# A planner that follows which bank is released first, and prices accumulator reads and narrow products

## The chip, the cores and the metric
The kernel runs on one core of one Trainium2 chip. The metric is the device time of one execution in microseconds. The core has five engines with queues of their own: PE (TensorE, with its weight loads shown as PEld), DVE (VectorE), ACT (ScalarE), POOL (GpSimd) and SP (SyncE, which here issues every DMA).

## The reference, cut to what matters
One layer of a hybrid decoder for a prompt of 512 tokens and for 8 decoding sequences of 4 new tokens each, all with D_MODEL 2048 in fp32:

```
z = rms_norm(x, g) @ w_in                      # 2048 -> 6144: q, k, v, g_A, u, g_B
a = dilated_prompt(q, k, v)                    # 16 heads x 64, three (window, dilation) patterns
a = dilated_sample(q, concat(cache_k, k), concat(cache_v, v), buf)   # the decoding rows
p = pool_mix(u)                                # trailing means over 2/4/8/16, 256x256 maps
h = x + concat(a * silu(g_A), p * silu(g_B)) @ w_out
y = rms_norm(h, final_norm_g)
# also returned: keys, values and pool history, among them the updated caches
# (8 x 2048 x 1024, keys and values), which are the old ones moved on by 4 rows
```

## The kernel before, in words
**Two stages.** The first stage multiplies the 544 tokens by w_in: 48 blocks of 128 output channels (`order`: q, k, v, g for eight head pairs, then u and p for the pooling), each the sum of 16 products over d. A product is three times two matmuls of 272 columns, since a weight and an input are each split into a high and a low part (`w_split`, `x_split`, `product`). Attention and pooling run in between. The second stage multiplies by w_out in 512-column blocks with all eight PSUM banks, then normalises and writes y.

**What is woven in.** The four main PSUM banks `mm` belong to the blocks (and to the pooling maps). Two banks, tag `aux`, serve everything else that PE does for the attention: `B`, query rows copied over the partitions for the decoding keys (`query_rows`, names `aux<-qm,oh`; DVE reads it in three multiplications `tmp<-kv,aux`, spread out over time); `S`, prompt scores (`prompt_scores`, `aux<-kHH,qS` and `aux<-kL,qS`; DVE reads it once, in `tensor_tensor_reduce`, which the profile calls CUSTOM_DVE_ANT_0 plus an accumulator read); `T`, transposed probabilities (`prompt_values`, `aux<-cst,P`; ACT copies it to `PT`); and transposes of new rows (`aux<-cst,zr`), of outputs (`aux<-cst,ov`) and of the decoding softmax. Banks `O` and `OS` collect attention outputs. The DMA side streams the caches through a ring `kv` of 7 buffers (plus one, `kvx`).

**What sets the order.** The program's order on each engine is fixed when the kernel is built, by a planner inside it. `Paced` wraps each engine: each call advances a modelled time `t` of that engine by a cost (`_pe_cost`, `_dve_cost`, `_act_cost`), not before its inputs are ready in the model (`Clock.ready`). Tasks are Python generators; `tick`, run after each product (`between`), resumes those whose condition holds at the modelled PE time `pe.t`. So an attention matmul takes its place in PE's in-order stream where the model says that its inputs will be there. `after(engine)` waits until `pe.t` has passed that engine's time plus MARGIN (0.4); `idle(dve)` waits until DVE's modelled backlog is under 0.2.

**Banks.** `bank()` first holds one of the two `aux` places (`hold`, by count), then makes the tile, then `vacant` waits until `pe.t` is past the time at which the model thinks that the tile's place came free, plus BANK (0.15). That time is the `floor` which `Clock.new` notes: the last recorded access of the tile made `bufs` tiles earlier in the same ring.

```
old = self.done[ring[-bufs]] if len(ring) >= bufs else ([], [])
floor = max([e[4] for es in old for e in es], default=0.0)
```

`kv_advance` asks `next_free` the same question of the `kv` ring before it issues a cache load on SP. `BULK_LEAD` paces 224 transfers that copy the caches from HBM to HBM: one is issued after a product while the modelled DMA time lies 2 us behind `pe.t`; those that are left are spread over the second stage.

Of the kernel before, what the change touches and what calls it, by code (L numbers as in the profile page):

```python
# [49 lines left out]
class Clock:  # L50
# [4 lines left out]
           ("POOL", "POOL"): 0.1}  # L55

    def __init__(self):
        self.done, self.rings = {}, {}

    def pool(self, pool, bufs=1):  # L60
        return PacedPool(self, pool, bufs)

    def new(self, t, bufs):
        ring = self.rings.setdefault(t.tensor.tag, [])
        old = self.done[ring[-bufs]] if len(ring) >= bufs else ([], [])
        floor = max([e[4] for es in old for e in es], default=0.0)
        ring.append(t.tensor.name)
        self.done[t.tensor.name] = ([(0, 128, 0, 1 << 30, floor, "")], [])

    def free(self, t):  # L70
        return self.done[t.tensor.name][0][0][4]

    def next_free(self, tag, bufs):

        ring = self.rings.get(tag, [])
        old = self.done[ring[-bufs]] if len(ring) >= bufs else ([], [])
        return max([e[4] for es in old for e in es], default=0.0)

    def box(self, x):
# [105 lines left out]
def _pe_cost(name, args, kw):  # L185
    n = _free(args[0])
    if name == "transpose":
        return 0.11
    if args[1].dtype == F32R:
        return 0.006 + max(n, 256) / 2264  # L190
    t = 4 * max(n, 64) / 2400
    return t / 4 if kw.get("tile_position") is not None else t / (2 if args[1].shape[-1] == 64 else 1)


def _dve_cost(name, args, kw):
    n = _free(args[1] if name == "tensor_reduce" else args[0])
    fast = name in ("tensor_scalar", "tensor_copy") and args[1].space != PSUM
    return 0.07 + n / (1920 if fast else 960) + (0.06 if name == "tensor_scalar" else 0.0)


def _act_cost(name, args, kw):
    t = _free(args[0]) / 1200 + (0.052 if args[1].space == PSUM else 0.094)
    if not isinstance(kw.get("scale", 1.0), float):
        t += 0.094
    return t + (0.094 if "accum_out" in kw else 0.0) + (0.094 if "bias" in kw else 0.0)


def _pool_cost(name, args, kw):
# [4 lines left out]
def kernel(ctx: ExitStack, tc: tile.TileContext, xT, xtok, ck, cv, stT, w_in, w_pool, w_out,  # L213
                           cst, fg, y, kpT, vpT, ppT, ks, vs, psT):
    nc = tc.nc
    clock = Clock()
# [35 lines left out]
    def bank(shape=(128, 512)):  # L252
        yield from hold("aux")
        b = px.tile(list(shape), F32, name="aux", bufs=2)
        yield from vacant(b)
        return b

    def vacant(t):
        free = clock.free(t)
# [109 lines left out]
    xr = {}  # L369
# [12 lines left out]
    def x_split(d):  # L382
        act.activation(xH[d], xr[d], AF.Copy, scale=gcol[:, d:d + 1])
        dve.scalar_tensor_tensor(xL[d], xr[d], gcol[:, d:d + 1], xH[d].bitcast(F32), ALU.mult, ALU.subtract)
        k = d % 2
        sq = sums[k] if d < 2 else per.tile([128, NT], F32, name="sq", tag=f"mixP{2 + d % 6}")
        act.activation(sq, xr[d], AF.Square)
        if d >= 2:
            squares.append((k, sq))

# [18 lines left out]
    def rstd_rows():  # L409
        yield after(dve, pool)  # L410
        b = yield from bank()
        for t in range(5):
            n = 128 if t < 4 else 32
            for k in range(2):
                pe.matmul(b[:n, t:t + 1], sums[k][:, 128 * t:128 * t + n], ones, start=(k == 0), stop=(k == 1))
        r5 = per.tile([128, 5], F32, name="r5")
        dve.memset(r5, 1.0)
        dve.tensor_copy(r5[:, 0:4], b[:, 0:4])
        dve.tensor_copy(r5[:32, 4:5], b[:32, 4:5])
        give("aux")  # L420
        pow_rstd(r5, r5, 128)
        yield after(pool)
        yield 1.5
        b = yield from bank()
        for t in range(4):
            pe.transpose(b[:, 128 * t:128 * t + 128], r5[:, t:t + 1].to_broadcast([128, 128]), ident)
        dve.tensor_copy(rstd[:, 0:512], b)
        give("aux")
        b = yield from bank()
        pe.transpose(b[:, 0:32], r5[:32, 4:5].to_broadcast([32, 128]), ident[:32, :32])  # L430
        dve.tensor_copy(rstd[:, 512:544], b[:, 0:32])
        give("aux")
        normed.append(1)

    normed = []
# [54 lines left out]
    def ev_q(p, ps):  # L490
        pr[p] = {"P": {}}
        z = yield from scaled(ps, -0.125)
        yield after(dve)
        Q, a = divmod(p, 2)
        b = yield from sample_rows(z)
        yield after(pe)
        if Q > 1 and Q - 2 not in softened:
            yield lambda: Q - 2 in softened
        qm = quad(Q)["q"]
        cols = slice(128 * a, 128 * a + 128)  # L500
        act.activation(qm[0:32, cols], b, AF.Copy)
        yield after(act)
        dve.tensor_tensor(qm[32:64, cols], b, qm[0:32, cols].bitcast(F32), ALU.subtract)
        give("aux")
        if a == 1:
            quad(Q)["ready"].add("q")
        st = []
        for s in range(2):
            o, n = 64 * s, 64 - 64 * s
            t = yield from slot("qS", F32R)  # L510
            act.activation(t[o:o + 64, :NP], z[o:o + 64, :NP], AF.Copy)
            st.append(t)
        yield after(act)
        for s in range(2):
            o, n = 64 * s, 64 - 64 * s
            dve.tensor_tensor(st[s][n:n + 64, :NP], z[o:o + 64, :NP], st[s][o:o + 64, :NP].bitcast(F32),
                              ALU.subtract)
        give("zr")
        pr[p]["qS"] = st

    def ev_k(p, ps):
# [3 lines left out]
        b = yield from sample_rows(z)  # L525
        yield after(pe)
        dve.tensor_copy(quad(Q)["k"][:, 128 * a:128 * a + 128], b)
        give("aux")
        if a == 1:
            yield after(dve)  # L530
            quad(Q)["ready"].add("k")
# [25 lines left out]
    def ev_v(p, ps):  # L557
        z = yield from scaled(ps)
        yield after(dve)
        Q, a = divmod(p, 2)  # L560
        b = yield from sample_rows(z)
        yield after(pe)
        dve.tensor_copy(quad(Q)["v"][:, 128 * a:128 * a + 128], b)
        give("aux")
        vt = yield from slot("vt")
        b = yield from bank()
        for j in range(4):
            pe.transpose(b[:, 128 * j:128 * j + 128], z[:, 128 * j:128 * j + 128], ident)
        yield after(pe)
        act.activation(vt[:, :NP], b, AF.Copy)  # L570
        give("aux")
        dma.start(nc.sync, vpT[128 * p:128 * p + 128, :], z[:, :NP])
        give("zr")
        yield after(act)
        pr[p]["vt"] = vt
        if a == 1:
            quad(Q)["ready"].add("v")
            kv_new()
            dma.start(nc.sync, vs[:, 2044:2048, 256 * Q:256 * Q + 256], quad(Q)["v"])
# [24 lines left out]
    def prompt_scores(p):  # L604
        st = pr[p]
        for i in range(4):
# [3 lines left out]
            for s in range(2):  # L610
# [4 lines left out]
                if i == 3:  # L615
# [5 lines left out]
                n = at.tile([128, 4], F32, name="n", bufs=6)  # L621
                dve.tensor_tensor_reduce(P[:, :nk], S[:, :nk], c[:, C_NBP + NP - nk:C_NBP + NP], 1.0, BIG,
                                         ALU.add, ALU.min, n[:, 0:1])
                give("aux")
                Ps.append(P)
                ns.append(n)
                yield after(dve)
# [9 lines left out]
    def prompt_values(p):  # L637
        st = pr[p]
        for i in range(4):
# [5 lines left out]
            for s in range(2):  # L645
                PT = yield from slot("PT")
                T = yield from bank()
                for j in range(i + 1):
                    pe.transpose(T[:, 128 * j:128 * j + 128], Ps[s][:, 128 * j:128 * j + 128], ident)
                give("P")  # L650
                yield after(pe)
                act.activation(PT[:, :nk], T[:, :nk], AF.Copy)
                give("aux")
                PTs.append(PT)
            yield after(act)
            if "vt" not in st:
# [43 lines left out]

    def kv_done(*ns):
        for n in ns:
            give(kv_tag.pop(n))

    def kv_load(n):
        Q, kv, b, h = parts[n]
# [1 line left out]
        cols = slice(256 * Q, 256 * Q + 256)  # L708
        tag = kv_next()
        taken[tag] += 1  # L710
        kv_tag[n] = tag
        if tag == "kvx":
            t = per.tile([128, NS, 256], F32, name="kvx", tag="mixP01")
        else:
# [4 lines left out]
            src = cache[b, 1536:1920, cols].rearrange("(a r) e -> a r e", r=4)  # L719
        else:  # L720
            src = cache[b:b + 4, 1920:2048, cols].rearrange("b r e -> r b e")
        kv_key[tag] = t.tensor.tag
        kv_time[n] = dma.start(nc.sync, t if h == 2 else t[0:96], src)
        kvt[n] = t
# [40 lines left out]
    def sample_all():  # L765
# [7 lines left out]
        for Q, kv, b in units:  # L773
# [7 lines left out]
            if kv == 0:  # L781
# [6 lines left out]
                for i in (0, 2):  # L788
# [5 lines left out]
                    for seg, nr, t in ((0, 96, tA), (1, 100, tB), (2, 128, tC)):  # L794
# [7 lines left out]
                        dve.tensor_tensor(tmp[:nr], kt, B[:nr], ALU.mult)  # L802
                        lo = 16 * b + 4 * i
                        pieces.append((SCs[Q][:nr, seg, lo:lo + 8], tmp[:nr].rearrange("p i (h d) -> p (i h) d", d=64)))
                    give("aux")
                kv_done(n, n + 1, *([nc4] if last else []))
                if b == NB - 1:
                    while pieces:
# [37 lines left out]
    def sample_softmax(Q):  # L846
# [10 lines left out]
        sb = lent("tmp")[:, :324]  # L857
        n = at.tile([128, 4], F32, name="n", bufs=6)
        dve.tensor_tensor_reduce(sb, T[:, :324], c[:, C_NBS:C_NBS + 324], 1.0, BIG, ALU.add, ALU.min, n[:, 0:1])
        give("aux")  # L860
        yield after(dve)
        act.activation(sb, sb, AF.Exp, bias=n[:, 0:1], scale=-1.0, accum_out=n[:, 1:2])
        yield after(act)
# [10 lines left out]
        act.activation(PA[:96, 0:128], T[:96, 0:128], AF.Copy)  # L874
        act.activation(PA[:100, 128:256], T[:100, 128:256], AF.Copy)
        act.activation(PA[:, 256:384], T[:, 256:384], AF.Copy)
        give("aux")
        yield after(act)
        sampled.add(Q)

# [2 lines left out]
    def sample_near(Q, b4, C):  # L883
# [1 line left out]
        yield after(pe)  # L885
        ov = sa.tile([128, 256], F32, name="ov", bufs=1)
        act.activation(ov, C, AF.Copy)
        give("aux")
        yield after(act)
        T = yield from bank()  # L890
        for k in range(2):
# [3 lines left out]
        for s in range(2):  # L895
# [1 line left out]
            Tb = T[lo:lo + 64, s:s + 255]  # L897
            dve.tensor_copy(mixS[lo:lo + 64, 2 * Q:2 * Q + 2, 4 * b4:4 * b4 + 16].rearrange("p k (j i) -> p k j i", i=NS),
                            bass.AP(tensor=Tb.tensor, offset=Tb.offset, ap=[Tb.ap[0], [130, 2], [32, 4], [4, 4]]))
        give("aux")  # L900
        near.add((Q, b4))

    def sample_out(Q, b2, O):
# [14 lines left out]
        for s in range(2):  # L918
# [3 lines left out]
            Tb = T[lo:lo + 64, s:s + 511]  # L922
            dve.tensor_tensor(o, bass.AP(tensor=Tb.tensor, offset=Tb.offset,
                                         ap=[Tb.ap[0], [130, 2], [256, 2], [32, 4]]), o, ALU.add)
        give("aux")
        for s in range(2):
            lo = 64 * s
            o = mixS[lo:lo + 64, 2 * Q:2 * Q + 2, at8]
# [463 lines left out]
```

## Time and profile before

| | us |
|---|---|
| median of 3 runs | 983.32 (982.81 to 984.39) |
| the profiled execution | 982.86 |
| its span, first to last instruction | 981.1 |
| PE busy in the span | 943.6 (96%) |
| DVE busy | 679.5 (69%) |
| ACT busy | 317.0 (32%) |

The span leaves out some 1.8 us at the ends of the execution. PE's busy time counts matmuls with modelled, overlapping ends, so a start-to-start distance says more of its rate than a duration does. All calls through the planner's wrapper carry line L149, all DMAs L174: the groups are told apart by the names of the tiles, as out<-in. A wait is put down to the instruction that ended it.

### The profile page before, as it was taken

The numbers are of one execution on the slowest core, as the hardware profiler recorded it, in microseconds if no ns is written. First come the engines' busy times: TensorE is split into PE (matmuls) and PEld (weight loads), VectorE is DVE, ScalarE is ACT, GpSimd is POOL, SyncE is SP. The second block draws the span as 40 slices with busy tenths as digits, with TensorE's granted clock in tenths as the row PEclk, the third lists the DMA queues.
The fourth block names the chain that finished last, engine by engine and source line by source line (L and its number), as shares of the span: only waits on it lengthen the run. The fifth ranks groups of instructions, "written<-read, shape, count | busy, mean of one in ns | idle before, by whom it ended". The sixth has DMA issues, their size and how long they took to land.

```text
span 981.1 us, 17768 instructions
## 1 busy us (share of the span) xinstructions
PE 943.6 (96%) x7097; PEld 841.5 (86%) x7097; DVE 679.5 (69%) x1362; ACT 317.0 (32%) x595; POOL 7.5 (1%) x20
## 2 busy tenths in 40 slices
PE   7999999999999899999999999999999999999995
PEld 7999989998888899898897899889999977777764
DVE  7654889898887798989877889753638635151524
ACT  8343332333332333422432322231222433131313
POOL 0000000000000000000000000000000000000002
PEclk9999999999999999999999999999999999999998
DMA  9989797788789789899977689899897899999954
GB/s 339 268 275 354 259 337 267 262 301 270 242 265 297 254 272 274 287 255 256 337 204 253 205 212 338 220 271 324 294 355 255 340 402 387 365 369 372 361 179 182
DMA packets 98978, 283.52 MB, mean 289 GB/s; under 512 B 12880, under 2 KB 71504, under 8 KB 94800
## 3 DMA queue, kind: packets, MB, share of 16 engines
q1 hardware_dynamic: 98896, 282.39, 86.4%
q8 instruction: 56, 0.92, 0.4%
q14 instruction: 26, 0.21, 0.1%
HBM read 271.84 MB, written 143.42 MB: 423 GB/s over the span
## 4 chain that ended last, share of the span: by engine, by line
PE 45%; DVE 5%; DMA 3%; ACT 1%; issue 1%; POOL 1%; SPq 0%; DVEq 0%; POOLq 0%; ACTq 0%
PE mm L149 30%; PE aux L149 8%; PE OS L149 4%; PE O L149 4%; DMA hist<-in_stT_dram 2%; DVE tmp L149 1%; DMA kv<-kvnew 1%; DVE SC L149 1%; DVE wL L149 1%; ACT wH L149 1%; DVE xt L149 1%; POOL rf L149 1%; SPq L174 0%; DVE P L149 0%; ACT junk L149 0%
## 5 line engine op out<-in xcount | busy, mean ns | idle before, releaser
L149 PE MATMUL mm<-xH,wH 128*128 128x272 f32 x1472 | 321.1, 299 | 6.7 <-ACT xH L149 6.5
L149 PE MATMUL mm<-xH,wL 128*128 128x272 f32 x1472 | 305.2, 289 | 0.0
L149 PE MATMUL mm<-xL,wH 128*128 128x272 f32 x1472 | 304.9, 289 | 0.0
L149 DVE TENSOR_TENSOR wL<-raw,wH 128x1024 fp32r<-128x1024 f32 (+1 forms) x128 | 154.1, 1207 | 200.5 <-ACT wH L149 200.0
L149 PEld LDWEIGHTS mm<-xH,wH 128*128 128x128 f32 x1472 | 230.4, 190 | 19.9 <-issue 12.0
L149 ACT ACTIVATE wH<-raw 128x1024 fp32r<-128x1024 f32 (+1 forms) x128 | 133.5, 1045 | 319.5 <-PE mm L149 168.2
L149 PEld LDWEIGHTS mm<-xL,wH 128*128 128x128 f32 x1472 | 232.0, 189 | 0.3 <-DVE xL L149 0.3
L149 PEld LDWEIGHTS mm<-xH,wL 128*128 128x128 f32 x1472 | 231.2, 189 | 0.0
L149 DVE TENSOR_REDUCE SC<-tmp 96x8 f32<-96x512 f32 (+2 forms) x192 | 126.2, 677 | 0.3
L149 DVE TENSOR_TENSOR tmp<-kv,aux 100x512 f32<-100x512 f32 (+2 forms) x168 | 111.6, 680 | 7.7 <-PE aux L149 6.3
L149 ACT ACTIVATE P<-P,n 128x128 f32<-128x128 f32 (+3 forms) x64 | 35.7, 558 | 94.4 <-DVE n L149 94.4
L149 ACT ACTIVATE PT<-aux 128x128 f32<-128x128 f32 (+3 forms) x64 | 27.6, 431 | 47.1 <-PE aux L149 46.7
L149 PE MATMUL aux<-cst,P 128*128 128x128 f32 x160 | 29.6, 283 | 12.0 <-DVE n L149 9.5
L149 DVE CUSTOM_DVE_ANT_0 P<-aux,cst 128x128 f32<-128x128 f32 (+3 forms) x64 | 31.0, 484 | 11.5 <-PE aux L149 11.1
L149 PE MATMUL mm<-wH,xH 128*128 128x512 f32 x96 | 38.7, 403 | 0.0
L149 PE MATMUL mm<-wH,xL 128*128 128x512 f32 x96 | 37.9, 394 | 0.0
L149 PE MATMUL mm<-wL,xH 128*128 128x512 f32 x96 | 37.8, 394 | 0.0
L149 PE MATMUL aux<-qm,oh 128*128 128x256 f32 x128 | 29.0, 308 | 6.5 <-DVE tmp L149 5.2
L149 PEld LDWEIGHTS aux<-cst,P 128*128 128x128 f32 x160 | 18.5, 140 | 17.9 <-DVE n L149 12.4
L149 PEld LDWEIGHTS aux<-qm,oh 128*128 128x128 f32 x128 | 19.5, 188 | 15.5 <-DVE tmp L149 5.3
L149 PE MATMUL aux<-wH,xH 128*128 128x512 f32 x80 | 31.9, 399 | 0.0
L149 PE MATMUL aux<-wH,xL 128*128 128x512 f32 x80 | 31.6, 395 | 0.0
(175 smaller groups left out, 1076.0 us busy)
## 6 DMA issues: line engine op xcount, KB each, us to landing
out_ks_dram<-in_ck_dram SPq DMA_DIRECT2D x112, 584.0 KB
out_vs_dram<-in_cv_dram SPq DMA_DIRECT2D x112, 584.0 KB
raw<-in_w_in_dram SPq DMA_DIRECT2D x94, 512.0 KB
kv<-in_cv_dram SPq DMA_DIRECT2D x58, 384.0 KB
kv<-in_ck_dram SPq DMA_DIRECT2D x56, 384.0 KB
raw<-in_w_out_dram SPq DMA_DIRECT2D x32, 512.0 KB
xt<-in_xtok_dram SPq DMA_DIRECT2D x4, 1024.0 KB
kv<-in_ck_dram SPq DMA_DIRECT2D x7, 512.0 KB
```

The source lines that it names most:

```text
L149: return f(*args, **kw)
```

## The change
It does three things. The clock notes, per ring, the order in which tiles are given back (`release`, `gone`), and `new` and `next_free` take the time of the tile that was given back first, not of the tile made `bufs` tiles earlier; `drop` replaces each `give("aux")`, and `kv_done` and `x_split` report theirs. PE products with a 64-column weight or a `tile_position` cost 0.03 more. On DVE `tensor_tensor_reduce` costs 0.08 more, and on ACT an accumulator output 0.187, not 0.094. No instruction's operands change.

```diff
     def new(self, t, bufs):
         ring = self.rings.setdefault(t.tensor.tag, [])
-        old = self.done[ring[-bufs]] if len(ring) >= bufs else ([], [])
-        floor = max([e[4] for es in old for e in es], default=0.0)
+        floor = self.next_free(t.tensor.tag, bufs)
+        gone = self.gone.get(t.tensor.tag)
+        if gone and len(ring) >= bufs:
+            gone.pop(0)
         ring.append(t.tensor.name)
...
+    def release(self, t):
+
+        self.gone.setdefault(t.tensor.tag, []).append(t.tensor.name)
+
     def next_free(self, tag, bufs):
 
         ring = self.rings.get(tag, [])
-        old = self.done[ring[-bufs]] if len(ring) >= bufs else ([], [])
+        if len(ring) < bufs:
+            return 0.0
+        gone = self.gone.get(tag)
+        old = self.done[gone[0] if gone else ring[-bufs]]
         return max([e[4] for es in old for e in es], default=0.0)
...
     t = 4 * max(n, 64) / 2400
-    return t / 4 if kw.get("tile_position") is not None else t / (2 if args[1].shape[-1] == 64 else 1)
+    if kw.get("tile_position") is not None:
+        return 0.03 + t / 4
+    return 0.03 + t / 2 if args[1].shape[-1] == 64 else t
...
-    return 0.07 + n / (1920 if fast else 960) + (0.06 if name == "tensor_scalar" else 0.0)
+    t = {"tensor_scalar": 0.06, "tensor_tensor_reduce": 0.08}.get(name, 0.0)
+    return 0.07 + n / (1920 if fast else 960) + t
...
-    return t + (0.094 if "accum_out" in kw else 0.0) + (0.094 if "bias" in kw else 0.0)
+    return t + (0.187 if "accum_out" in kw else 0.0) + (0.094 if "bias" in kw else 0.0)
...
+    def drop(b):
+        give("aux")
+        clock.release(b)
...
         act.activation(sq, xr[d], AF.Square)
+        if d > len(early):
+            clock.release(xr[d])
...
     def kv_done(*ns):
         for n in ns:
-            give(kv_tag.pop(n))
+            tag, t = kv_tag.pop(n)
+            give(tag)
+            if tag == "kv":
+                clock.release(t)
```

## Rows read from the trace of the kernel before

**Rows 1.** The page: busy time by engine, and the granted PE clock by slice.
```profile
PE 943.6 (96%) x7097; PEld 841.5 (86%) x7097; DVE 679.5 (69%) x1362; ACT 317.0 (32%) x595; POOL 7.5 (1%) x20
...
PEclk9999999999999999999999999999999999999998
```

**Rows 2.** Stretches: PE, PEld, DVE, ACT, POOL busy (count); clock, DMA share, GB/s.
```profile
300.00:350.00 50.00, 46.32 (x392) 41.52 (x391) 39.39 (x88) 16.07 (x37) 0.00 (x0) 1.00 0.79 257
...
sum 550.00, PE 530.36 PEld 485.99 DVE 464.96 ACT 175.39 POOL 0.00; mean PE 48.21 PEld 44.18 DVE 42.27 ACT 15.94 POOL 0.00
...
673.00:774.00 101.00, 100.78 (x802) 100.51 (x802) 57.08 (x131) 26.89 (x41) 0.00 (x0) 1.00 0.87 306
```

**Rows 3.** PE's waits from 100 to 650 us: total us, times, longest.
```profile
PE aux L149 <- DVE n L149: 10.6, 10, 1.6
PE aux L149 <- DVE tmp L149: 5.2, 7, 1.2
PE aux L149 <- ACT PT L149: 1.9, 4, 0.7
```

**Rows 4.** Timeline around one wait: start, duration, engine, instructions, idle before.
```profile
131.05 0.40 PE L149 MATMUL aux<-qm,oh 128*128 128x256 f32 x2
...
132.81 0.39 PE L149 MATMUL aux<-kHH,qS 128*128 128x512 f32 x1
...
133.77 0.41 PE L149 MATMUL mm<-xH,wL 128*128 128x272 f32 x2
133.84 1.23 DVE L149 TENSOR_TENSOR wL<-raw,wH 128x1024 fp32r<-128x1024 f32 x1 [1.46 <-ACT wH L149]
134.99 0.68 DVE L149 CUSTOM_DVE_ANT_0 P<-aux,cst 128x512 f32<-128x512 f32 x1
...
135.59 1.28 DVE L149 TENSOR_TENSOR tmp<-kv,aux 96x512 f32<-96x512 f32 x2
...
135.74 0.55 PE L149 MATMUL aux<-cst,P 128*128 128x128 f32 x3 [1.56 <-DVE n L149]
```

**Rows 5.** Timeline: the first wait of this kind, and the last of 26.
```profile
107.98 0.40 PE L149 MATMUL aux<-qm,oh 128*128 128x256 f32 x2
...
113.31 0.27 PE L149 MATMUL aux<-cst,P 128*128 128x128 f32 x1
...
114.99 0.47 PE L149 MATMUL aux<-qm,oh 128*128 128x256 f32 x2 [0.55 <-DVE tmp L149]
...
559.11 0.50 PE L149 MATMUL aux<-qm,oh 128*128 128x256 f32 x2 [0.31 <-DVE tmp L149]
```

**Rows 6.** Groups by form: count, busy us, mean ns, idle before.
```profile
L149 ACT ACTIVATION_READ_ACCUMULATOR P<-P,n 128x1 f32 x64 | 12.0, 187 | 0.0
L149 ACT ACTIVATE P<-P,n 128x512 f32<-128x512 f32 x16 | 11.5, 717 | 16.7 <-DVE n L149 16.7
...
L149 DVE CUSTOM_DVE_ANT_0 P<-aux,cst 128x512 f32<-128x512 f32 x16 | 10.9, 684 | 3.7 <-PE aux L149 3.7
```

**Rows 7.** Timeline: a group of 64-column products, and PE's next start.
```profile
147.82 1.09 PE L149 MATMUL O<-PT,vt 128*64 128x128 f32 x16
...
148.84 0.50 PE L149 MATMUL aux<-qm,oh 128*128 128x256 f32 x2
```

**Rows 8.** Stretches of the second stage, columns as in the second group.
```profile
890.00:920.00 30.00, 30.00 (x136) 22.50 (x135) 6.55 (x7) 6.20 (x8) 0.00 (x0) 1.00 1.01 370
...
950.00:955.00 5.00, 5.00 (x30) 2.75 (x29) 2.01 (x3) 1.06 (x1) 0.00 (x0) 1.00 0.00 0
```

**Rows 9.** Waits of SP's queue over the whole span: total us, times, longest.
```profile
SPq L174 <- DVE tmp L149: 126.3, 31, 10.2
```

**Rows 10.** Timeline: last scores of one head pair, and the next pair's conversion.
```profile
139.46 0.40 PE L149 MATMUL aux<-kHH,qS 128*128 128x512 f32 x1
...
147.35 1.27 ACT L149 ACTIVATE qS<-zr 64x512 fp32r<-64x512 f32 x2
```

More of the change, by code (lines that the diff above doesn't have):

```diff
@@ L57, in __init__ @@
     def __init__(self):
-        self.done, self.rings = {}, {}
+        self.done, self.rings, self.gone = {}, {}, {}
     def pool(self, pool, bufs=1):
@@ L419, in rstd_rows @@
         dve.tensor_copy(r5[:32, 4:5], b[:32, 4:5])
-        give("aux")
+        drop(b)
         pow_rstd(r5, r5, 128)
@@ L427, in rstd_rows @@
         dve.tensor_copy(rstd[:, 0:512], b)
-        give("aux")
+        drop(b)
         b = yield from bank()
@@ L431, in rstd_rows @@
         dve.tensor_copy(rstd[:, 512:544], b[:, 0:32])
-        give("aux")
+        drop(b)
         normed.append(1)
@@ L503, in ev_q @@
         dve.tensor_tensor(qm[32:64, cols], b, qm[0:32, cols].bitcast(F32), ALU.subtract)
-        give("aux")
+        drop(b)
         if a == 1:
@@ L527, in ev_k @@
         dve.tensor_copy(quad(Q)["k"][:, 128 * a:128 * a + 128], b)
-        give("aux")
+        drop(b)
         if a == 1:
@@ L563, in ev_v @@
         dve.tensor_copy(quad(Q)["v"][:, 128 * a:128 * a + 128], b)
-        give("aux")
+        drop(b)
         vt = yield from slot("vt")
@@ L570, in ev_v @@
         act.activation(vt[:, :NP], b, AF.Copy)
-        give("aux")
+        drop(b)
         dma.start(nc.sync, vpT[128 * p:128 * p + 128, :], z[:, :NP])
@@ L623, in prompt_scores @@
                                          ALU.add, ALU.min, n[:, 0:1])
-                give("aux")
+                drop(S)
                 Ps.append(P)
@@ L652, in prompt_values @@
                 act.activation(PT[:, :nk], T[:, :nk], AF.Copy)
-                give("aux")
+                drop(T)
                 PTs.append(PT)
@@ L710, in kv_load @@
         taken[tag] += 1
-        kv_tag[n] = tag
         if tag == "kvx":
@@ L721, in kv_load @@
             src = cache[b:b + 4, 1920:2048, cols].rearrange("b r e -> r b e")
+        kv_tag[n] = tag, t
         kv_key[tag] = t.tensor.tag
@@ L804, in sample_all @@
                         pieces.append((SCs[Q][:nr, seg, lo:lo + 8], tmp[:nr].rearrange("p i (h d) -> p (i h) d", d=64)))
-                    give("aux")
+                    drop(B)
                 kv_done(n, n + 1, *([nc4] if last else []))
@@ L859, in sample_softmax @@
         dve.tensor_tensor_reduce(sb, T[:, :324], c[:, C_NBS:C_NBS + 324], 1.0, BIG, ALU.add, ALU.min, n[:, 0:1])
-        give("aux")
+        drop(T)
         yield after(dve)
@@ L876, in sample_softmax @@
         act.activation(PA[:, 256:384], T[:, 256:384], AF.Copy)
-        give("aux")
+        drop(T)
         yield after(act)
@@ L887, in sample_near @@
         act.activation(ov, C, AF.Copy)
-        give("aux")
+        drop(C)
         yield after(act)
@@ L899, in sample_near @@
                             bass.AP(tensor=Tb.tensor, offset=Tb.offset, ap=[Tb.ap[0], [130, 2], [32, 4], [4, 4]]))
-        give("aux")
+        drop(T)
         near.add((Q, b4))
@@ L924, in sample_out @@
                                          ap=[Tb.ap[0], [130, 2], [256, 2], [32, 4]]), o, ALU.add)
-        give("aux")
+        drop(T)
         for s in range(2):
```

## The prediction
> **What bounds the kernel now.** I read the page first: PE is busy for 943.6 of 981.1 us, DVE for 679.5 [rows 1]. So the kernel can only lose what PE stands still, 37.5 us. The table of stretches shows where. From 100 to 650 us, while attention is woven into the projection, PE is busy for 530.36 of 550, so it stands for 19.64; from 673 us to the end of the projection at 774 it is busy for 100.78 of 101 [rows 2]. The rest lies before the first product and behind the last matmul, which the change doesn't touch. PE's waits name the 19.64: 10.6 us for "DVE n" (the accumulator read behind the score reduction), 5.2 for "DVE tmp", 1.9 for "ACT PT", 17.7 together, nearly all in front of instructions that write `aux` [rows 3]. These wait for a bank, not for operands: the transposes at 135.74 need probabilities of an older step, yet start just as the reduction of *other* scores lets go.
>
> The timeline shows how [rows 4]. B is made at 131.05, S at 132.81, T starts at 135.74. B is still to be read by two multiplications that begin at 135.59, so T can only have S's bank, whose reader runs from 134.99 to 135.67. The planner asked after the tile two places back, B, whose recorded accesses were all old, and let T into PE's stream at once. The last product matmul began near 133.90 (second of the pair at 133.77), and another could have followed 0.125 later: PE stood for 135.74 - 133.90 - 0.125 = 1.72 us (the idle time shown, 1.56, is less because the modelled end of the matmul covers some).
>
> **How much of it is this error.** I followed both banks through the timeline: each group of PE instructions that writes `aux`, with its last reader, gives 265 tiles with a known place. In 160 the place that came free first is not that of the tile two back. At least 0.25 us late are 29 starts. 26 of them are among the 160, from 114.99 to 559.11, and stand 22.6 us start to start. At 114.99 B takes the bank of the B of 107.98, released at 114.84, while the planner followed the T of 113.31 [rows 5]. Two of the other three wait for operands, and one is a tile judged by the right place that was late by 0.57. Of the 105 judged rightly, only this one stood for its bank. Starts under 0.25 us late add some 1.2 among the 160: 23.8 us in reach.
>
> **The change, part by part.**
> *Release order for `aux`.* No instruction is added or removed, only places in the stream move. T of [rows 4] would enter once `pe.t` passes S's modelled end plus 0.15, and two or three products of 6 x 0.125 = 0.75 us go ahead of it. They are the block's own, ready and due anyway, so the stall becomes work done. Behind T on PE wait only later products; on ACT its copy, and then the O products, which come about a product later. Bounds: nothing is gained if the model is late anyway; all 23.8 if it is exact. I take 20.8 out and 0.8 back: the 160 will stall as the 105 did, 0.57/105 each, is 0.9, but the 105 were easy (nine in ten had their place free for over 0.4 us), so I keep three times that, 3 us, for residual error, and 23.8 - 3 is 20.8. The 0.8 is for the next part.
>
> *Costs.* On 512 columns the model gave the reduction 0.07 + 512/960 = 0.60 and now gives 0.68; the row says 0.684. For the exponential it gave 0.094 + 0.427 + 0.094 + 0.094 = 0.71 and now 0.80; the rows say 0.717 and an accumulator read of 0.187 that starts before the first ends [rows 6]. Both make S's release and the probabilities later in the model by what they are late on the chip, which is what the waiting tile needs. The 64-column products go from 0.107 to 0.137; sixteen records (eight products, two passes each) took 148.84 - 147.82 = 1.02, 0.128 each [rows 7]. The 32-column ones I take at the same estimate, the nearest row. There are 160 + 288 of them, so `pe.t` gains 448 x 0.03 = 13.4 us over the first stage. This takes away a hidden margin: a tile behind eight such products was let in 8 x 0.03 = 0.24 us later in real time than the model meant. Some 3 of 160 tiles may lose 0.25 by it: 0.8 us, between 0 and 4 if it were one in ten.
>
> *Order for `kv`.* SP stands 126.3 us in 31 waits for DVE to release a cache buffer [rows 9], and every transfer behind stands with it. With the right place the load is issued later and bulk copies go ahead. PE gains nothing: none of its waits is for a transfer [rows 3]. If this cover went, a late cache load would show as DVE waiting, and B's bank held longer; I price it 0 to 3 us of loss, and take 0.
>
> *Bulk copies.* The pacing by `pe.t` lets 13.4 us more of modelled time: at 598,016 bytes by the model's 390 GB/s, 1.53 us each, up to 8 more copies in the first stage, 8 fewer in the second. There the DMA share is 1.01 with PE at 30.00 of 30, and from 950 to 955 it is 0.00 [rows 8]: fewer cost nothing, and eight more would fit into the hole before the output. In the first stage the share (0.79 from 300 to 350, 0.87 at its end [rows 2]) rises by a few hundredths. Worth 0.
>
> *Sum.* 982.86 (profiled execution) - 20.8 + 0.8 = 962.9. The median shown is 0.46 above that execution, so 963.3; I say 963.
>
> **Two rules weighed.** The granted clock is at its upper level, 2.4 GHz, in every stretch, with waits of 1.6 us in them [rows 1, 2]. The Trainium skill (TensorE: Matmul & The Clock Gate, "A second HAM failure mode: psum-queue depth-cycling") says that short idle times between groups that cycle through PSUM banks can make the clock swing and cost throughput. By it, taking the waits out would give back more than their length; by the rows there is nothing to give back, and the sum stays.
>
> **Rivals.**
> *Half.* The right place is followed, but its time is too early: DVE's queue runs later than modelled, as when the weight split at 133.84 waited 1.46 us for ACT [rows 4]. For it: the reader itself was late there; against: that wait is in the model too, and 104 of 105 tiles did well. With half of 23.8 gone: 971.
>
> *The bubble stays.* With two banks T can't start before S is read, wherever it stands. If PE reached the end of the ready products while it waited, it would stand as before: 983. Against it: the blocks follow on each other without a gap where no `aux` tile stands in between, 100.78 of 101 [rows 2]. The Trainium skill (Perfetto Trace Analysis, "Optimization Strategy") reads the same gap repeated on the engine that should be saturated as a possible lack of SBUF or PSUM for the next tile, which would make order powerless; the trace agrees that banks are short, and not that PE lacks other work.
>
> *Slower: the prompt chain becomes the pace.* Tiles now wait for a product boundary, 0.15 + 0.75/2, is 0.5 us behind a release. A head pair's last scores at 139.46 free `qS` for the next pair's conversion at 147.35, 8 us of room [rows 10]. The 44 tiles that now start within 0.1 us of a release cost 44 x 0.5 / 8 = 2.8 us a pair, and PE's 20 us less over 8 pairs another 2.5: 5.3 of 8. It decides from 8 on. If all 20 misjudged tiles of a pair were late by 0.9, 18 us, each pair would fall back 10 further, 80 us in all; held z buffers carry three blocks (96 x 0.125 = 12 us each and what is woven in, 50 us by estimate), then PE stands at block starts for 30: 983 - 20 + 30, is 993. Against it: most of the 160 had a free place long before.
>
> **How the numbers follow.** As sum 0.64, with a range of its own of 957 to 968; half 0.18 (969 to 976); bubble stays 0.08 (981 to 985); slower 0.10 (986 to 995). The range 957 to 976 holds the first two, 0.82; the floor is 982.86 - 23.8, a little less for chance. A difference under 0.2% can't be told from none. Faster: 0.64 + 0.18 + 0.02 of the third = 0.84; same 0.06; slower 0.10.
>
> **What would show it.** PE's waits for `aux` fall from 17.7 us to about 3, and PE stands for about 4 from 100 to 650 instead of 19.64, with the same 7097 instructions. The projection ends near 754 instead of 774, and from there to the end the time is unchanged. SP's waits for "DVE tmp" fall. Wrong would be: waits for "DVE n" still near 10 (half, or the bubble), or PE waiting in front of `mm` blocks for DVE's z (the slower rival).

## The result and the profile after

The changed kernel takes 968.38 us (median of 4 runs, 966.28 to 970.71) against 983.65 of the kernel before: a ratio of 0.9846, 95% interval 0.982 to 0.9872. By the medians 15.3 us are gained. The profiled execution takes 969.34 us with a span of 967.5, so that span is 13.6 us shorter. The helper's lines have moved to L158 (engines) and L183 (DMAs).

PE's waits from 100 to 650 us, which answer to [rows 3]:

```profile
PE aux L158 <- ACT ov L158: 3.1, 1, 3.1
PE aux L158 <- DVE tmp L158: 1.4, 4, 0.4
PE aux L158 <- DMA kv<-in_cv_dram: 0.9, 1, 0.9
PE OS L158 <- DMA kv<-kvnew: 0.9, 1, 0.9
PE aux L158 <- DVE n L158: 0.5, 2, 0.3
PE aux L158 <- DVE mixS L158: 0.3, 1, 0.3
```

The waits for a bank are what is left of "DVE n" (10.6 to 0.5), "DVE tmp" (5.2 to 1.4) and "ACT PT" (1.9 to none). New are 3.1 us for ACT ("ACT ov") and twice 0.9 for a transfer. The stretches tell where these lie. First the kernel before, then the changed one; the columns are those of [rows 2].

```profile
100.00:590.00 490.00, 471.13 (x3942) 432.84 (x3942) 419.46 (x872) 160.16 (x334) 0.00 (x0) 1.00 0.83 265
590.00:660.00 70.00, 69.22 (x622) 61.41 (x621) 51.20 (x116) 18.87 (x37) 0.00 (x0) 1.00 0.97 273
```
```profile
100.00:590.00 490.00, 487.52 (x4112) 453.10 (x4111) 438.56 (x908) 167.48 (x343) 0.00 (x0) 1.00 0.91 291
590.00:660.00 70.00, 64.78 (x589) 55.33 (x588) 38.00 (x98) 17.08 (x35) 0.00 (x0) 1.00 0.90 257
660.00:758.00 98.00, 97.78 (x780) 97.59 (x780) 55.16 (x126) 25.47 (x37) 0.00 (x0) 1.00 0.89 312
```

Up to 590 us PE's idle time falls from 490 - 471.13 = 18.87 us to 2.48, and PE gets through 4112 matmuls there instead of 3942: 170 more, at 0.125 us each some 21 us of work. From 590 to 660 it rises from 0.78 to 5.22, and 589 matmuls run instead of 622. So about the predicted 20 us were gained between 100 and 590, and some 4.4 us of idle time (5.22 - 0.78) came back in the 70 us that follow.

In this execution another 1.6 us were lost before 100 us, and not to a wait. First the kernel before, then the changed one:

```profile
0.00:60.00 60.00, 52.86 (x398) 51.83 (x399) 41.94 (x75) 35.41 (x61) 2.10 (x10) 1.00 0.89 281
```
```profile
0.00:60.00 60.00, 53.00 (x384) 51.74 (x385) 40.66 (x73) 35.22 (x59) 2.10 (x10) 0.97 0.85 269
```

The granted clock (the last column but two) stood at its lower level, 1.2 GHz, for a few us around 40 us: from 30 to 50 us PE, busy throughout, ran 151 matmuls instead of 164, and 13 at 0.125 us are 1.6 us. This comes and goes between executions of one kernel: below, two profiles of the same kernel ran 152 and 164 matmuls there, and the kernel before with only its history copy moved, at a later place, ran 152. So it is no effect of the change.

The step of [rows 4] in the changed kernel: S at 133.45, its reduction from 134.89 to 135.57, T at 136.18, and PE never stands in between.

```profile
133.45 0.40 PE L158 MATMUL aux<-kHH,qS 128*128 128x512 f32 x1
...
133.74 1.23 DVE L158 TENSOR_TENSOR wL<-raw,wH 128x1024 fp32r<-128x1024 f32 x1 [0.84 <-ACT wH L158]
...
134.89 0.68 DVE L158 CUSTOM_DVE_ANT_0 P<-aux,cst 128x512 f32<-128x512 f32 x1
...
135.92 0.41 PE L158 MATMUL mm<-xH,wL 128*128 128x272 f32 x2
...
136.18 0.49 PE L158 MATMUL aux<-cst,P 128*128 128x128 f32 x3
```

The reduction waits for the same weight split as before; T is now placed behind the reduction in PE's stream, with block products ahead of it.

The longest of the new waits, the 3.1 us, comes from ACT, from 618 to 632 us (ACT's timeline, then SP's):

```profile
618.28 0.39 ACT L158 ACTIVATE ov<-OS 128x256 f32<-128x256 f32 x1 [1.37 <-PE aux L158]
629.30 0.31 ACT L158 ACTIVATE US<-hist 128x120 f32<-128x120 f32 x1 [10.63 <-DMA hist<-in_stT_dram]
629.64 0.31 ACT L158 ACTIVATE hist<-US 128x120 f32<-128x120 f32 x1
629.85 1.04 ACT L158 ACTIVATE wH<-raw 128x1024 fp32r<-128x1024 f32 x1
630.80 0.36 ACT L158 ACTIVATE ov<-aux 128x256 f32<-128x256 f32 x1
```
```profile
613.24 3.95 SPq L183 DMA_DIRECT2D kv<-in_cv_dram  x3
618.16 0.70 SPq L183 DMA_DIRECT2D kv<-kvnew  x1
...
620.17 0.35 SPq L183 DMA_DIRECT2D hist<-in_stT_dram  x1
622.14 0.34 SPq L183 DMA_DIRECT2D out_ppT_dram<-qS  x1
629.97 0.34 SPq L183 DMA_DIRECT2D out_psT_dram<-hist  x1
630.41 1.09 SPq L183 DMA_DIRECT2D kv<-in_cv_dram  x2
```

`ev_u` loads the pooling history at 620.17 and, 3 us of modelled time later, puts ACT's copy of it (`US<-hist`) into ACT's stream. The copy starts 9.1 us after the load's issue. ACT stands 10.63 us in front of the copy, and behind it wait the next weight split and the copy `ov<-aux`, for which PE stands until 631.22. SP has next in its queue the store of the history, which needs ACT's second instruction, so nothing is issued from 622.5 to 629.97, and the cache loads come after that. The two waits of 0.9 us for transfers are another matter. They end at 622.57 and 625.02, and SP issued what they wait for at 618.16 and by 617.2, before the history load.

### The profile page after: what moved, and what is told of

Read it like the earlier page. It is cut to its first block, busy times and chain, and to the rows that moved or that the text cites. A ratio compares the mean times of both kernels' runs of the same rounds, so it can differ in the third digit from the quotient of the medians.

```text
span 967.5 us, 17765 instructions
## 1 busy us (share of the span) xinstructions
PE 942.1 (97%) x7097; PEld 843.7 (87%) x7097; DVE 678.9 (70%) x1362; ACT 318.7 (33%) x595; POOL 7.6 (1%) x20
## 4 chain that ended last, share of the span: by engine, by line
PE 81%; DMA 7%; DVE 6%; issue 2%; ACT 1%; SPq 1%; POOL 1%; DVEq 0%; POOLq 0%; ACTq 0%
PE mm L158 57%; PE aux L158 14%; PE O L158 6%; PE OS L158 5%; DMA hist<-in_stT_dram 3%; DMA kv<-in_cv_dram 2%; DMA raw<-in_w_in_dram 1%; DVE wL L158 1%; DVE tmp L158 1%; DVE kL L158 1%; DMA xr<-in_xT_dram 1%; SPq L183 1%; DVE xt L158 1%; ACT wH L158 1%; POOL rf L158 1%
## 5 line engine op out<-in xcount | busy, mean ns | idle before, releaser
L158 PE MATMUL mm<-xH,wH 128*128 128x272 f32 x1472 | 320.7, 299 | 6.0 <-ACT xH L158 5.7
L158 PE MATMUL mm<-xL,wH 128*128 128x272 f32 x1472 | 305.2, 289 | 0.1
L158 PE MATMUL mm<-xH,wL 128*128 128x272 f32 x1472 | 305.2, 289 | 0.0
L158 DVE TENSOR_TENSOR wL<-raw,wH 128x1024 fp32r<-128x1024 f32 (+1 forms) x128 | 154.0, 1206 | 201.3 <-ACT wH L158 198.4
L158 PEld LDWEIGHTS mm<-xH,wH 128*128 128x128 f32 x1472 | 230.5, 190 | 18.5 <-issue 11.4
L158 PEld LDWEIGHTS mm<-xL,wH 128*128 128x128 f32 x1472 | 231.9, 189 | 0.7 <-DVE xL L158 0.7
L158 ACT ACTIVATE wH<-raw 128x1024 fp32r<-128x1024 f32 (+1 forms) x128 | 133.5, 1045 | 299.5 <-PE mm L158 161.0
L158 PEld LDWEIGHTS mm<-xH,wL 128*128 128x128 f32 x1472 | 231.3, 189 | 0.0
L158 DVE TENSOR_REDUCE SC<-tmp 96x8 f32<-96x512 f32 (+2 forms) x192 | 126.1, 677 | 0.3
L158 DVE TENSOR_TENSOR tmp<-kv,aux 100x512 f32<-100x512 f32 (+2 forms) x168 | 111.2, 680 | 3.5 <-PE aux L158 1.9
L158 ACT ACTIVATE P<-P,n 128x128 f32<-128x128 f32 (+3 forms) x64 | 35.8, 560 | 115.9 <-DVE n L158 115.9
L158 PE MATMUL mm<-wH,xH 128*128 128x512 f32 x96 | 38.7, 403 | 0.0
L158 ACT ACTIVATE PT<-aux 128x128 f32<-128x128 f32 (+3 forms) x64 | 27.6, 432 | 32.1 <-PE aux L158 31.5
L158 PE MATMUL mm<-wH,xL 128*128 128x512 f32 x96 | 37.9, 394 | 0.0
L158 PE MATMUL mm<-wL,xH 128*128 128x512 f32 x96 | 37.8, 394 | 0.0
L158 DVE CUSTOM_DVE_ANT_0 P<-aux,cst 128x128 f32<-128x128 f32 (+3 forms) x64 | 30.9, 483 | 6.3 <-PE aux L158 6.1
L158 PE MATMUL OS<-kv,PA 96*32 96x256 f32 (+1 forms) x464 | 31.7, 384 | 0.9 <-DMA kv<-kvnew 0.9
L158 PE MATMUL aux<-wH,xH 128*128 128x512 f32 x80 | 31.9, 399 | 0.0
L158 PE MATMUL aux<-wH,xL 128*128 128x512 f32 x80 | 31.6, 395 | 0.0
L158 PE MATMUL aux<-wL,xH 128*128 128x512 f32 x80 | 31.5, 394 | 0.0
L158 PE MATMUL aux<-qm,oh 128*128 128x256 f32 x128 | 29.7, 313 | 1.6 <-DVE tmp L158 1.0
L158 PEld LDWEIGHTS aux<-qm,oh 128*128 128x128 f32 x128 | 19.3, 188 | 11.3 <-issue 4.2
```

What stands on the lines that cost most here:

```text
L158: return f(*args, **kw)
```

## The experiments

"Changed" and "before" are the two kernels above. Each ratio is against the kernel before, on the same chip.

**One part at a time.** Aux order alone: `release` and `next_free` as changed, without the two reports for the cache ring, and with the four old costs.

```diff
-        if d > len(early):
-            clock.release(xr[d])
...
-            if tag == "kv":
-                clock.release(t)
...
-    if kw.get("tile_position") is not None:
-        return 0.03 + t / 4
-    return 0.03 + t / 2 if args[1].shape[-1] == 64 else t
+    return t / 4 if kw.get("tile_position") is not None else t / (2 if args[1].shape[-1] == 64 else 1)
...
-    t = {"tensor_scalar": 0.06, "tensor_tensor_reduce": 0.08}.get(name, 0.0)
+    t = {"tensor_scalar": 0.06}.get(name, 0.0)
...
-    return t + (0.187 if "accum_out" in kw else 0.0) + (0.094 if "bias" in kw else 0.0)
+    return t + (0.094 if "accum_out" in kw else 0.0) + (0.094 if "bias" in kw else 0.0)
```

> Only the release order of the two aux banks; the cache ring and all costs are as before. If the wrong place of a bank was the cause (my account), PE's waits for aux fall from 17.7 us to under 5 and the time comes to 964 to 971, near the changed kernel's 968. If the added costs did it (rival), it stays at 979 to 984 with PE's waits for 'DVE n' near 10 us. If both are needed, about 975.

Measured: 965.79 us, ratio 0.9811 (0.9791 to 0.983). One part gives the whole gain. Its ratio is a little below that of the full change, 0.9846, and the intervals overlap. PE stands for 490 - 488.13 = 1.87 us from 100 to 590, against 18.87 before.

Costs alone: the four costs stay, both rings are followed as before (the edit is against the changed kernel, as all are unless the text says otherwise).

```diff
     def drop(b):
         give("aux")
-        clock.release(b)
...
-        if d > len(early):
-            clock.release(xr[d])
...
-            if tag == "kv":
-                clock.release(t)
```

> Only the four added costs; banks and cache ring are followed as before. My account: tiles are still let in after the wrong tile, PE's waits for aux stay at 13 to 20 us, time 980 to 985. Rival (the costs did it): 966 to 972 with waits under 6 us.

Measured: 996.49 us, ratio 1.0116 (1.01 to 1.0131). The waits are there as expected, but it is slower than either account said. PE's waits over the whole span:

```profile
PE aux L158 <- DVE n L158: 10.2, 8, 1.6
PE aux L158 <- DVE tmp L158: 6.6, 8, 2.4
...
PE aux L158 <- ACT PT L158: 3.5, 6, 0.7
PE aux L158 <- ACT ov L158: 2.9, 1, 2.9
```

The bank waits of [rows 3] stand (10.2, 6.6, 3.5), and the wait of 2.9 for "ACT ov", with 16.1 us of ACT standing for history loads between 590 and 680, is of the kind seen above. So finer costs removed no wait, and this order ran into the history load too (tested below).

Cache ring as before: the changed kernel without the first two hunks of the diff of the aux order.

> The changed kernel with the cache ring followed as before. My account: PE waits for no transfer because of it, so 966 to 971 as the changed kernel, unless the late transfers at 615 to 631 us come from the cache loads being issued later, in which case it is faster, 960 to 964, and PE stands for under 2 us from 600 to 650 instead of 5.2.

Measured: 972.99 us, ratio 0.9876 (0.9858 to 0.9894). It lies outside both expectations, and is neither faster than the changed kernel nor plainly equal to it. Up to 570 us its waits are those of the changed kernel, one for one; then PE waits 4.5 us for DVE's softmax of the decoding scores, while ACT stands 9.3 us for a history load and DVE behind ACT. That the cache order is worth something by itself can't be read from this while the history wait differs.

**The history load.** One number in the changed kernel: ACT's copy is placed 8 us after the load.

```diff
         give("mm")
-        yield 3.0
+        yield 8.0
         act.activation(US[:, :, 0:15], hist, AF.Copy)
```

> The changed kernel; ACT's copy of the pooling history is placed 8 us after its load instead of 3. Account: between 600 and 650 us ACT stood 10.6 us for that load, SP stood behind ACT's result, the cache loads behind it on SP came late, and PE lost some 8 us to this; so the time falls to 958 to 964 and PE's idle time from 600 to 650 from 5.2 to under 2. Rival: the transfers are late whatever ACT does (the DMA engines are behind), then 966 to 971 and PE's waits for kv stay.

Measured: 962.37 us, ratio 0.9775 (0.9753 to 0.9798), as my account had it. In its profiled execution, the slowest of the four (965.64), PE still waits 2.4 us for rows copied in behind a cache load, so late transfers don't hang on the history wait. One step of my account is not borne out, that the cache loads behind the history load came late for PE: in the changed kernel's profile PE waits for none of the loads issued after 629.97.

The same edit in the kernel before:

> The kernel before, with ACT's copy of the pooling history placed 8 us after its load instead of 3: the control for the history copy in the changed kernel. If that wait cost the kernel before as much (rival), it gains some 7 us, 975 to 979. If the cost is new, because the changed order runs into it, it gains 0 to 3 us, 980 to 985, with PE's waits for aux in front of the attention tiles still 15 to 19 us.

Measured: 984.8 us, ratio 0.9998 (0.9988 to 1.0007): nothing. The kernel before had ACT stand 6.6 us for the same load, but no PE work hung on it.

The edit with the aux order alone:

> Release order of the aux banks alone, and the later history copy; costs and cache ring as before. Account: the two effects add, and costs and cache order are worth nothing, so 957 to 963, equal to the changed kernel with the later copy within 3 us. Rival: the costs or the cache order are worth some 4 us, then 964 to 968.

Measured: 964.28 us, ratio 0.9798 (0.9783 to 0.9813). The time lies at the lower edge of the rival's range; the distance to the changed kernel with the later copy, 0.0023 of the time (2 us), is within the 3 us of my account. The intervals of the two kernels overlap, so the costs and the cache order together are not told apart from nothing.

**Two tries at the transfers.** With the later copy, a later start behind each cache load:

```diff
-KV_LAG = 2.0
+KV_LAG = 4.0
```

> The changed kernel with the later history copy, and 4 us instead of 2 after the modelled landing of a cache load. It stood for 2.4 us in two waits for rows that are copied behind a cache load; this should take them out: 958 to 962, PE waits for no transfer. Rival: the later start of each unit makes the attention end later and hides nothing, 963 to 968.

Measured: 965.19 us, ratio 0.9806 (0.9781 to 0.9832). A miss: no better than 2 us of lag, and PE still waits 1.5 and 0.5 us for transfers.

The bulk copies paced further behind PE, in the changed kernel:

```diff
-BULK_LEAD = -2.0
+BULK_LEAD = -8.0
```

> The changed kernel with the bulk copies paced 8 us behind the modelled PE time instead of 2. If the transfers at 600 to 650 us come late because bulk copies sit in front of them (rival to the history account), PE's idle time there falls from 5.2 to under 2 us and the time to 960 to 964. If it is ACT and SP standing behind the history load, whose own latency of 9 us the pacing hardly changes, 966 to 971.

Measured: 1130.17 us, ratio 1.1479 (1.1461 to 1.1496). A miss, and of the edit rather than of the account: I took the number for a fixed distance, but the modelled DMA time is moved up by every cache load, so it is seldom 8 us behind `pe.t` and few bulk copies are issued. From 100 to 590 us 9 are issued, where the changed kernel issues 94. The others fall to the second stage, from 780 us on:

```profile
780.00:1128.00 348.00, 208.55 (x807) 145.53 (x805) 74.58 (x99) 47.36 (x74) 5.45 (x10) 0.79 0.98 342
```

PE is busy for 208.55 of 348 us at a DMA share of 0.98. So the bulk copies cost nothing only as long as PE's work in the first stage covers them. The trace does bear on the history wait all the same. No bulk copy is issued from 500 to 620 us, and still ACT stands 9.0 us for the history load, and PE as long as before for ACT:

```profile
PE aux L158 <- ACT ov L158: 2.9, 1, 2.9
```

So bulk copies in front of the load are not what makes it long.

**All of it side by side**, four kernels on one chip. The changed kernel once more:

> The changed kernel itself once more, as the measure for the other three on the same chip. 966 to 971, ratio 0.982 to 0.987; PE idle from 100 to 590 us about 2.5, from 590 to 660 about 5 again if the history wait belongs to this order and is not chance.

Measured: 969.49 us, ratio 0.984 (0.982 to 0.986). ACT waits 8.49 us for the history at the same place, PE 2.8 us for "ACT ov".

With the later copy, once more:

> The changed kernel with the later history copy, once more: 961 to 965, below the run of the changed kernel beside it by 4 to 8 us, if the wait for the history load is what kept the gain from 20 us. Rival (the difference seen before was chance between chips): within 2 us of it.

Measured: 962.34 us, ratio 0.9777 (0.9759 to 0.9796). The difference to the run beside it is 7.15 us by the medians, and the two intervals do not overlap. Its two stretches, the same as above, and the waits of ACT for the history from 590 to 660:

```profile
100.00:590.00 490.00, 487.56 (x4112) 453.16 (x4111) 438.54 (x909) 166.10 (x341) 0.00 (x0) 1.00 0.92 296
590.00:660.00 70.00, 70.00 (x635) 61.36 (x635) 40.23 (x100) 18.58 (x36) 0.00 (x0) 1.00 0.97 286
```
```profile
ACT US L158 <- DMA hist<-in_stT_dram: 0.5, 1, 0.5
```

From 100 to 590 us nothing differs from the changed kernel (487.56 and 487.52), and from 590 to 660 PE is busy throughout.

Not all of the 7.15 us is the history wait. The two profiled spans differ by 7.5 us: 3.2 are PE's idle time from 590 to 660 in the changed kernel, some 1.4 the lower clock there (0.02 of 70 us), and 1.6 the lower clock around 40 us, which the changed kernel's profile has (151 matmuls from 30 to 50 us) and this one has not (164). The first profile of this same kernel, under "The history load", has it too (152). The rest, some 1 us, I can't place. Without the chance part the later copy is worth 5 to 6 us, by estimate. And PE's late transfers (0.9 and 0.9 us in the changed kernel, none in its repeat, 2.4 with the later copy, none in its repeat) come and go between executions.

The later copy, with the cache ring followed as before:

> The changed kernel with the later history copy and the cache ring followed as before. If the cache order is worth nothing by itself (my prediction) and its absence cost 4 us only through a longer wait for the history load, it equals the kernel with the cache order beside it within 2 us, 961 to 966. If the cache order itself helps (rival), it is 4 us slower, 966 to 969.

Measured: 961.86 us, ratio 0.977 (0.9752 to 0.9788), equal to the kernel beside it. So the cache order is worth nothing that the runs can tell here, and what its absence had cost went with the history wait.

The costs alone, with the later copy:

> The four costs alone, old release order, and the later history copy. If the costs alone were 11 us slower because their order ran into the history load, this comes back to 983 to 988. If finer costs hurt by themselves while the wrong tile is followed (rival: tiles are let in 0.24 us closer), it stays at 992 to 997 with PE's waits for aux in front of attention tiles at 18 us or more.

Measured: 986.82 us, ratio 1.0021 (1.0011 to 1.0031). Of the 11 us that the costs alone lost, 9 or so went with the later copy. What is left, 0.2%, is small but clear of the interval: while the wrong tile is followed, finer costs don't help and may hurt a little. Its waits for banks are the old ones:

```profile
PE aux L158 <- DVE n L158: 10.2, 8, 1.6
...
PE aux L158 <- DVE tmp L158: 4.2, 7, 0.9
PE aux L158 <- ACT PT L158: 3.5, 6, 0.7
```

## Why the prediction was right, and where it was short

**The bound and the cause were right.** PE's 19.64 us of idle time were the loss that could be won back, and the wrong place of a bank was the cause: order alone takes the waits away, costs alone leave them. "The bubble stays" is refuted by T at 136.18 and by 170 more matmuls in the same 490 us.

**The main term was right in size.** 23.8 - 3 for the bank waits: idle time up to 590 falls by 18.87 - 2.48 = 16.4 us, and a wait is longer start to start than as shown (by 0.16 at 135.74). With the later copy the two runs measure 984.3 - 962.34 = 21.96 us of gain, against the 20 of the sum; in the kernel before the later copy alone gains nothing (0.9998). The waits for banks that remain, 1.4 + 0.5 + 0.3 = 2.2 us, compare with the 3 that I kept for residual error.

**The costs came out at about nothing**, as in the sum (0.8 us of loss), but not for my reason. I held them useful to the waiting tile; with the order right, leaving them out loses nothing that the runs can tell (0.9811 without, 0.9846 and 0.984 with; 0.9798 and 0.9777 with the later copy). The 0.8 us for the lost margin is below what the runs can tell.

**The cache order was worth 0, as said, but one sign was wrong.** SP's waits for "DVE tmp" did not fall [rows 9]:

```profile
SPq L183 <- DVE tmp L158: 133.6, 34, 10.1
```

Why SP still stands there with the right place followed was not tested.

**The step that failed is "PE gains nothing: none of its waits is for a transfer".** From the same rows I concluded that no transfer could hold PE later. I read PE's waits alone and not those of the engines that feed it. ACT's waits for history loads were in the profile of before (590 to 660 us), harmless there:

```profile
ACT US L149 <- DMA hist<-in_stT_dram: 11.2, 2, 6.6
```

When the same attention work came earlier, a copy that PE needs and a weight split stood in ACT's queue behind such a load. PE lost 3.1 us directly in the profiled execution (2.8 in the repeat); placing the copy later gave back 7.15 us side by side, 5 to 6 without the chance part. None of my rivals had this mechanism.

It is not all that the forecast of 963 missed. PE's idle time from 590 to 660, 5.22 us, is about what lies between 963 and 968.38; 3.1 of it is the history wait, and 1.8 the two transfers issued before that load. The profiled execution, 969.34, also has the 1.6 us of lower clock, which the forecast, made from an execution without it, could not hold. Waits for transfers put at nothing are thus the other part of the step that failed.

The sum's own range ended at 968. The whole range held because it reached to the "half" case, whose cause (banks read too early) did not occur: that part was luck. The sign that I gave, PE standing for about 4 us from 100 to 650, did not come either: it stands for 7.7, of which 2.5 lie before 590.

The rest followed. The last product with w_in begins at 758.13 and began at 771.65 before (the 774 of the prediction was the end of a stretch, 2 us past it). PE is as busy from 660 us to there as it was before (97.78 of 98 us), and from that product to the end of the span it is 209.4 us in both.

**The slower rival** did not come: no block waits for z, and the time is shorter. Costs alone show that a slower outcome was within reach of this planner, by the same history wait.

## What to carry to other kernels

When a program of fixed order is planned against a model, check first whether the model follows the right resource, and only then how fine its prices are: here the order alone gave 1.9% and the prices alone cost 0.2 to 1.2%. A wait on an engine that is off the critical path can cost nothing until a change of order puts needed work behind it: look in the profile for in-order instructions that stand long in front of a load, and ask what would be behind them if the work came earlier. The kernel that is best by these runs is the changed one with the history copy 8 us after its load, 0.9777 of the kernel before (0.9759 to 0.9796); without the cache order it is as fast (0.977).

## What the runs showed that was not expected

A load of 60 KB took 9.1 us from its issue to the copy that waited for it, while the DMA share of the stretch was 0.90, and a fixed delay of 3 us in the planner had stood for it.

The granted clock fell to its lower level at different places, and the length of PE's wait just before does not tell when. In the changed kernel's repeat a wait of 2.8 us ended at 629.6, and the mean of the stretch from 590 to 660 us is 0.98; with the aux order alone it is 0.98 too, after a wait of 1.7 us. In the changed kernel's first profile a wait of 3.1 us at the same place left it at 1.00, and 25 waits of up to 1.6 us left every stretch of the kernel before at 1.00. Why is open, as it is for the lower clock around 40 us, where PE was busy throughout.

```profile
590.00:660.00 70.00, 66.79 (x594) 57.75 (x593) 38.66 (x98) 17.06 (x35) 0.00 (x0) 0.98 0.90 262
```
